# The modulation in the first feed-forward: one step behind each tile, the split's subtractions on VectorE, VectorE's order written out

## The chip, the cores and the metric

The kernel runs on one core of one Trainium2 chip. The metric is the device time of one execution in microseconds, the median of several runs. The core has five engines that take their own instructions in order: TensorE (PE; PEld is its weight load), VectorE (DVE), ScalarE (ACT), GpSimd (POOL) and SyncE (SP), which issues the loads.

## What is computed

Two transformer blocks on 512 tokens of 1024 features, in float32. The first block takes its norms' shifts, scales and gates from a vector `c`:

```python
c_act = jax.nn.silu(c)
mod = c_act @ w_mod[l] + b_mod[l]                       # 1024 x 9216
sh1, sc1, ga1, sh2, sc2, ga2, sh3, sc3, ga3 = jnp.split(mod, 9, axis=-1)
h = modulate(rms_norm(x, g_ffn1[l]), sh1, sc1)
x = x + 0.5 * (1 + ga1) * swiglu(h, w1_gate[l], w1_up[l], w1_down[l])   # D_FF = 2816
h = modulate(rms_norm(x, g_mix[l]), sh2, sc2)
x = x + (1 + ga2) * hybrid_mixer(h, ...)
h = modulate(rms_norm(x, g_ffn2[l]), sh3, sc3)
x = x + 0.5 * (1 + ga3) * swiglu(h, w2_gate[l], w2_up[l], w2_down[l])
```

The second block (a mixer and 64 experts) is not touched.

## The kernel before

Activations lie transposed, features in the partitions, 512 tokens in the columns. Every float32 product is made of three (`mm3`, L73): both operands are split in a high and a low part. A weight panel is loaded into `wraw`, ScalarE rounds it to `wh` (L105) and GpSimd subtracts, `wl` (L110); there are four buffers of each. The hidden size 2816 is 22 tiles of 128, f = 0 to 21, in four groups (0 to 5, 6 to 11, 12 to 16, 17 to 21). In `ffn` (L473) a tile is two times 24 products of 512 columns, gate and up, into PSUM (`at`, six banks). ScalarE takes the silu of the gate (L504), VectorE multiplies by the up half (L505), ScalarE makes the high part `ah` (L87), VectorE the low part `al` (L88). After a group come its down products: eight feature tiles, each 3 products per hidden tile, added to `xT` by VectorE (L517). The products of tiles 0 and 1 are made earlier, in `first_norm`.

The first feed-forward also computes seven of the nine chunks of the modulation, in 14 halves of 512 columns; such a half is called an item here. `between(f)`, called behind each tile from f = 2 on, does one: `load_mod` (L230) loads 2 MB of `w_mod` in two tiles `wmod` (four buffers); `mod_rows` (L240) sums over the eight feature tiles with c as a factor, one operation L255 and seven L257 on VectorE, in `modacc`; `thirds` (L260) splits the sum in three bfloat16 parts:

```python
nc.scalar.activation(parts[0], x, AF.Copy)
nc.gpsimd.tensor_sub(x, x, parts[0])
nc.scalar.activation(parts[1], x, AF.Copy)
nc.gpsimd.tensor_sub(parts[2], x, parts[1])
```

and `mod_cols` (L270) sums these over the partitions with twelve products of one column on TensorE, adds the bias (L280) and makes A (L285) or G (L287) of it. The gates G of the first feed-forward (the first two items) are needed by its first down products.

Within `ffn` of the first feed-forward no order is written out: a scheduler sets the order on each engine from the order in the code and what it reckons to be ready. On VectorE it lets the row operations of several items run ahead of the tile that they stand behind in the code.

Of the kernel before, what the change touches and what calls it, by code (L numbers as in the profile page):

```python
# [17 lines left out]
P = 128  # L18
# [7 lines left out]
# rows of the table of per-feature vectors, 128 features a row  # L26
# [8 lines left out]
class Net:  # L35
# [37 lines left out]
    def mm3(self, out, lh, ll, rh, rl, start, stop, open_=False):  # L73
        """float32 product from operands split in two 12-bit parts."""
        self.mm(out, lh, rh, start, False, open_)
        self.mm(out, lh, rl, False, False, open_)
        self.mm(out, ll, rh, False, stop, open_)

    def split(self, h, l, src, scale=None, pool=False):
        """h + l = scale * src, in two 12-bit parts; pool: the second on GpSimd (src in SBUF)."""  # L80
# [12 lines left out]
    def panel(self, loads, cols=1024, into=None):  # L93
        """Weights of up to [128, 1024] from DRAM, split for mm3."""
# [18 lines left out]
    def kpanel(self, src, nk, nc_, into=None):  # L113
        """src: [nk*128, nc_] in DRAM -> ([128, nk, nc_]) x 2"""
# [7 lines left out]
    def setup(self):  # L122
# [10 lines left out]
        # one table set with both Exp and Ln  # L133
        nc.scalar.preload_act_table_set("natural_log_exp_and_others")

    def load_rows(self, lo, hi):
        """Rows lo to hi of the table of vectors"""
# [13 lines left out]
    def columns(self, rows, lo, hi):  # L151
        """Rows of the table, transposed"""
# [4 lines left out]
    def silu_c(self, pool, cr):  # L157
        """silu(c) with 31 columns of zeros after each"""
# [3 lines left out]
        # c / (1 + exp(-c))  # L162
# [11 lines left out]
    def transpose_x(self, xr, j, into):  # L174
        """Feature tile j of natural tiles (in two halves), transposed"""
# [7 lines left out]
    def copy(self, i, out, src):  # L183
        """On ScalarE and VectorE in turn"""
        if i % 2:
            self.nc.scalar.activation(out, src, AF.Copy)
        else:
            self.nc.vector.tensor_copy(out, src)
# [5 lines left out]
    def in_order(self):  # L194
        """Every engine takes the block's instructions in the order they are written in."""
# [4 lines left out]
    def order(self, n0, only=None):  # L200
        """Issue order for what was traced since n0, of all engines or of one"""
# [10 lines left out]
    def behind(self):  # L212
        """What is traced in the block comes after all that was traced before, on each engine."""
# [6 lines left out]
    def scale_x(self, pool, xr, t, xs):  # L220
        """A tile of x / rms(x), natural"""
# [18 lines left out]
    def mod_rows(self, pool, rs, on_pe=False):  # L240
        """Half of the columns of one of the nine chunks of silu(c) * w_mod, to be summed over the partitions."""
        nc = self.nc
        acc = self.sb(pool, [P, 512], F32, "modacc", 2)
        if on_pe:
            # the four column groups of the array take two of the eight feature tiles each
# [14 lines left out]
    def thirds(self, pool, x):  # L260
        """Three bfloat16 parts of x"""
        nc = self.nc
        parts = [self.sb(pool, [P, 512], BF16, f"third{i}", 2) for i in range(3)]
        nc.scalar.activation(parts[0], x, AF.Copy)
        nc.gpsimd.tensor_sub(x, x, parts[0])
        nc.scalar.activation(parts[1], x, AF.Copy)
        nc.gpsimd.tensor_sub(parts[2], x, parts[1])
        return parts

    def mod_cols(self, chunk, half, parts):  # L270
        """The sums of all parts, transposed, + b_mod; A = gain * (1 + scale) and G = (1 + gate) or half of it"""
# [17 lines left out]
    def rstd(self, ssum, n, width, parts=P, r=None):  # L289
        """1 / sqrt(ssum / n + eps)"""  # L290
# [6 lines left out]
    def newton(self, r, ssum, n, t, u):  # L297
        """A step towards 1 / sqrt(ssum / n + eps): r * (1.5 - 0.5 * (ssum / n + eps) * r^2)"""
# [7 lines left out]
    HALVES = (slice(0, 256), slice(256, 512))  # L306

    def square(self, j, half, acc):
        """acc += xT[j] ** 2"""
# [7 lines left out]
    def norm_half(self, half, acc, acol, bcol, off, hs, between=lambda j: None):  # L317
        """hidden = rms(xT) * acol + bcol, split; written from column off of the hidden tiles."""
# [21 lines left out]
    def norm_after(self, steps, ahead, acol, bcol, off=0):  # L340
        """steps[half]: (j, function that updates that half of xT[j]). Returns the hidden tiles, of which the
        first half of the tokens is there, and a function that makes the second."""
# [14 lines left out]
    def pe_order(self):  # L357
        """The products from norm_after's first on, in the order they are written in"""
        self.order(self.pe_order_from, mybir.EngineType.PE)

    def use_exp(self):
        """The one table set with both Exp and Ln, for all that follows"""
# [6 lines left out]
    def first_norm(self, pool, wg, wu):  # L369
        """The first norm and modulation, in two halves of the features, and the first products, which take the first  # L370
        half while the second's modulation comes in. Returns the hidden tiles and the products."""
# [101 lines left out]
    def ffn(self, pool, i, wg, wu, wd, nxt, hs=None, second=None, between=lambda f: None):  # L473
        """hs, second: hidden tiles from norm_after; nxt: the next norm's columns. Returns the next norm_after."""
        nc = self.nc
        groups = ((0, 6), (6, 12), (12, 17), (17, 22))
        if i == 0:
            hs, done = self.first_norm(pool, wg, wu)
        else:
# [8 lines left out]
            self.pe_order()  # L488
        for f0, f1 in groups:
# [32 lines left out]
            if f1 < NF:  # L522
                for j in range(KD):
                    down(j, load(j), slice(0, S))
        self.use_exp()
        # the panels of the last four stay for the second half of the tokens
# [13 lines left out]
    def mixer_consts(self, pool):  # L540
        """Triangles, masks and selectors that depend on positions alone."""
# [5 lines left out]
        # tri[j', j] = -1 where j' >= j  # L547
# [4 lines left out]
        # ones within a head of 64, for two heads  # L552
# [6 lines left out]
        # query i (partition), key j: 0 where j <= i  # L559
# [4 lines left out]
        # key j (partition), query i: 0 where i > j  # L564
# [4 lines left out]
        # sel[32*part + h, h, :] = 1  # L569
# [11 lines left out]
    def values(self, pool, hs, w, c0, tag, second=None):  # L581
        """Natural [token, 512 features] of hidden @ w[:, c0:c0+512], the two parts of a head's 64 side by side"""
# [1499 lines left out]
```

## Time and profile before

| | |
|---|---|
| three runs | 2341.15, 2341.27, 2341.89 us; median 2341.27 |
| profiled execution, span | 2341.2 us |
| TensorE busy | 2111.6 us, 90% |
| VectorE, ScalarE, GpSimd busy | 886.0, 596.2, 649.5 us |
| first feed-forward's tiles and down products, about 44 to 456 us of the span: TensorE busy | 377.4 of 411.6 us |

The profiled execution's own time is its span, and it stands 0.1 us from the median. Busy time is the union of an engine's instructions; an instruction's time includes what it stands still inside. A wait is the idle time in front of an instruction, put down to what ended it.

### The profile page before, as it was taken

How to read it: one execution, taken by the hardware profiler on the slowest of the kernel's cores; microseconds unless marked ns; L12 is line 12 of the kernel's file. 1: busy time of each engine (PE TensorE's matmuls, PEld its weight loads, DVE VectorE, ACT ScalarE, POOL GpSimd, SP SyncE). 2: the span in 40 equal slices, each digit the busy share in tenths (PEclk: the TensorE clock that was granted, in tenths of full speed). 3: DMA queues.
4: the chain of work that ended last, by engine and by line, in shares of the span. 5: the costliest groups of instructions: out<-in, count | busy, mean ns of one | idle time of the engine just before them, and what ended most of it. 6: DMA issues, size and time to landing. Idle time of an engine off the chain costs nothing.

```text
span 2341.2 us, 28454 instructions
## 1 busy us (share of the span) xinstructions
PE 2111.6 (90%) x11561; PEld 1387.7 (59%) x11561; DVE 886.0 (38%) x1390; ACT 596.2 (25%) x1027; POOL 649.5 (28%) x415
## 2 busy tenths in 40 slices
PE   8899899899888999999899999988888599888886
PEld 5677788788767888888897764333333143333332
DVE  5958322757588522122735562111111111111112
ACT  4322222455265322223434430000000000000002
POOL 2655444575532444444535400000000000000001
PEclk9999999999999999999999999999999799999998
DMA  9676323321211232332432099999999999999998
GB/s 327 218 247 210 96 81 88 106 64 47 72 45 37 78 103 86 104 89 85 108 87 86 15 364 399 420 421 420 421 421 421 377 421 421 420 421 421 420 421 310
DMA packets 275915, 550.05 MB, mean 235 GB/s; under 512 B 18461, under 2 KB 199862, under 8 KB 228678
## 3 DMA queue, kind: packets, MB, share of 16 engines
q1 hardware_dynamic: 272832, 547.78, 62.2%
q8 instruction: 92, 1.51, 0.3%
q10 hardware_dynamic: 2950, 0.43, 0.1%
q14 instruction: 41, 0.34, 0.0%
HBM read 546.06 MB, written 2.10 MB: 234 GB/s over the span
## 4 chain that ended last, share of the span: by engine, by line
PE 47%; DMA 36%; DVE 11%; ACT 3%; issue 2%; POOL 1%; SPq 0%; POOLq 0%; ACTq 0%; DVEq 0%
PE at L71 32%; PE mm L71 15%; DMA ew<-in_expert_w_gate 12%; DMA ew<-in_expert_w_down 11%; DMA ew<-in_expert_w_up 11%; DVE modacc L257 3%; DMA wmod<-in_w_mod 1%; DVE tmp L314 1%; DVE tmp L329 0%; POOL wl L110 0%; DVE al L88 0%; DVE hl L337 0%; DVE hd L88 0%; DVE pd L690 0%; DVE pc L689 0%
## 5 line engine op out<-in xcount | busy, mean ns | idle before, releaser
L110 POOL TENSOR_TENSOR wl<-wraw,wh 128x1024 fp32r<-128x1024 f32 (+3 forms) x216 | 476.2, 2207 | 512.6 <-ACT wh L105 491.7
L71 PE MATMUL at<-ew,xg 128*32 128x512 f32 x2048 | 330.6, 644 | 72.7 <-DMA ew<-in_expert_w_up 45.9
L71 PE MATMUL at<-hh,wh 128*128 128x512 f32 (+3 forms) x800 | 301.4, 381 | 3.2 <-ACT hh L420 2.4
L71 PE MATMUL at<-hl,wh 128*128 128x512 f32 (+3 forms) x800 | 301.0, 381 | 2.3 <-DVE hl L337 2.3
L105 ACT ACTIVATE wh<-wraw 128x1024 fp32r<-128x1024 f32 (+2 forms) x193 | 183.8, 954 | 456.5 <-PE mm L71 161.4
L71 PE MATMUL at<-hh,wl 128*128 128x512 f32 (+3 forms) x800 | 299.0, 379 | 0.0
L1779 POOL TENSOR_TENSOR sg<-oh,Gt 128x512 f32<-128x512 f32 x16 | 16.8, 1047 | 853.2 <-PE at L1831 507.5
L71 PEld LDWEIGHTS at<-ew,xg 128*32 128x32 f32 x2048 | 74.9, 116 | 285.6 <-issue 139.4
L71 PE MATMUL at<-ew,ehT 128*32 128x512 f32 (+1 forms) x1040 | 185.2, 596 | 19.3 <-ACT ehT L1843 10.4
L71 PE MATMUL mm<-ah,wh 128*128 128x512 f32 (+1 forms) x432 | 155.7, 360 | 36.0 <-ACT ah L87 20.2
L71 PEld LDWEIGHTS at<-hh,wh 128*128 128x128 f32 (+1 forms) x800 | 150.8, 189 | 37.1 <-ACT hh L420 4.8
L71 PEld LDWEIGHTS at<-hl,wh 128*128 128x128 f32 (+1 forms) x800 | 151.1, 189 | 32.6 <-DVE hl L337 3.0
L71 PEld LDWEIGHTS at<-hh,wl 128*128 128x128 f32 (+1 forms) x800 | 151.8, 190 | 28.7
L71 PEld LDWEIGHTS at<-oh,xn 128*128 128x128 f32 x1024 | 123.2, 197 | 72.9 <-issue 70.5
L71 PE MATMUL mm<-al,wh 128*128 128x512 f32 (+1 forms) x432 | 154.5, 358 | 1.8 <-DVE al L88 1.8
L71 PE MATMUL at<-oh,xn 128*128 128x128 f32 x1024 | 135.3, 287 | 21.1 <-DMA ew<-in_expert_w_gate 19.7
L71 PE MATMUL mm<-ah,wl 128*128 128x512 f32 (+1 forms) x432 | 153.6, 355 | 0.0
L1866 DVE TENSOR_TENSOR ewa<-ewa,mm 128x512 f32<-128x512 f32 (+1 forms) x124 | 83.0, 670 | 168.5 <-PE mm L71 168.4
L1838 DVE SCALAR_TENSOR_TENSOR eh<-at,rslot,eh 128x512 f32<-128x512 f32 x16 | 17.4, 1085 | 324.3 <-PE at L71 324.3
L71 PE MATMUL mm<-ey,sgT 128*128 128x512 f32 (+1 forms) x264 | 125.0, 604 | 2.0 <-DVE ewa L1869 0.8
L505 DVE TENSOR_TENSOR silu<-at,silu 128x512 f32<-128x512 f32 x44 | 30.3, 689 | 253.6 <-PE at L71 245.7
L1791 DVE TENSOR_TENSOR xg<-at,gexp 128x512 f32<-128x512 f32 x31 | 21.5, 692 | 274.9 <-PE at L71 274.9
(483 smaller groups left out, 3203.1 us busy)
## 6 DMA issues: line engine op xcount, KB each, us to landing
ew<-in_expert_w_gate SPq DMA_DIRECT2D x128, 1024.0 KB, 19.8
ew<-in_expert_w_up SPq DMA_DIRECT2D x128, 1024.0 KB, 19.8
ew<-in_expert_w_down SPq DMA_DIRECT2D x122, 1024.0 KB, 19.8
wmod<-in_w_mod SPq DMA_DIRECT2D x36, 1024.0 KB, 8.2
wraw<-in_w_gate SPq DMA_DIRECT2D x44, 512.0 KB, 3.9
wraw<-in_w_up SPq DMA_DIRECT2D x44, 512.0 KB, 3.9
wraw<-in_w_in SPq DMA_DIRECT2D x39, 512.0 KB, 3.8
wraw<-in_w_down SPq DMA_DIRECT2D x40, 320.0 KB, 3.1
```

The source lines that it names most:

```text
L71: self.nc.tensor.matmul(out, lhsT, rhs, start=start, stop=stop, skip_group_check=open_)
L105: self.nc.scalar.activation(h[:, :cols], r[:, :cols], AF.Copy)
L110: (eng or self.nc.gpsimd).tensor_sub(l[:, :cols], r[:, :cols], f32(h[:, :cols]))
L257: nc.vector.scalar_tensor_tensor(acc, r, c, acc, op0=ALU.mult, op1=ALU.add)
L314: self.nc.vector.tensor_add(acc, acc, sq)
L505: nc.vector.tensor_mul(s, ps[1], s)
L1779: nc.gpsimd.tensor_tensor(sg.rearrange("p t (e s) -> p t e s", s=self.CAP), ov, self.G[:, :, es_].unsqueeze(3).to_broadcast(shp), op=ALU.mult)
L1791: nc.vector.tensor_tensor(xg[:, half * 4:half * 4 + 4], px.rearrange("p (j c) -> p j c", c=P), gain, op=ALU.mult)
L1838: nc.vector.scalar_tensor_tensor(hf, pu, rs, hf, op0=ALU.mult, op1=ALU.mult)
L1866: nc.vector.tensor_add(self.acc[t][:, cs], self.acc[t][:, cs], pc[:, :w])
```

## The change

`thirds` goes. A new function `modulation` does an item in three steps, behind three tiles one after the other: row operations, ScalarE's parts and the first subtraction behind tile f; the second subtraction behind the next tile; `mod_cols` behind the one after. Both subtractions are on VectorE. The loads of an item are written behind the row operations of the item before it, those of the first behind tile 0. Items start behind tiles 1 to 4, 6 to 10, 12 to 15 and 17; behind 5, 11, 16, 20 and 21 no item starts, but what is under way goes on. In the first feed-forward VectorE's instructions from tile 0 to the last tile's are held in the order in which they are written. Comments and docstrings have gone from the file too, and lines have moved: L505 is now L524, L517 L536, L265 L280, L267 L271, L264 L279, L266 L281, L280 L296, L285 L301, L287 L303.

```diff
-    def thirds(self, pool, x):
-        nc = self.nc
-        parts = [self.sb(pool, [P, 512], BF16, f"third{i}", 2) for i in range(3)]
-        nc.scalar.activation(parts[0], x, AF.Copy)
-        nc.gpsimd.tensor_sub(x, x, parts[0])
-        nc.scalar.activation(parts[1], x, AF.Copy)
-        nc.gpsimd.tensor_sub(parts[2], x, parts[1])
-        return parts
+    def modulation(self, pool, todo):
+        nc = self.nc
+        loads, split, cols = [self.load_mod(pool, *todo[0])], [], []
+
+        def step(start=True):
+            if cols:
+                self.mod_cols(*cols.pop(0))
+            if split:
+                chunk, half, x, parts = split.pop(0)
+                nc.vector.tensor_sub(parts[2], x, parts[1])
+                cols.append((chunk, half, parts))
+            if start and todo:
+                chunk, half = todo.pop(0)
+                x = self.mod_rows(pool, loads.pop(0))
+                if todo:
+                    loads.append(self.load_mod(pool, *todo[0]))
+                parts = [self.sb(pool, [P, 512], BF16, f"third{i}", 2) for i in range(3)]
+                nc.scalar.activation(parts[0], x, AF.Copy)
+                nc.vector.tensor_sub(x, x, parts[0])
+                nc.scalar.activation(parts[1], x, AF.Copy)
+                split.append((chunk, half, x, parts))
+
+        return step
...
     def ffn(self, pool, i, wg, wu, wd, nxt, hs=None, second=None, between=lambda f: None):
...
+        if i == 0:
+            n0 = len(self.traced())
         for f0, f1 in groups:
...
+        if i == 0:
+            self.order(n0, mybir.EngineType.DVE)
         self.use_exp()
...
                 def between(f):
-                    if f > 1 and rest:
-                        c, h = rest.pop(0)
-                        n.mod_cols(c, h, n.thirds(p, n.mod_rows(p, n.load_mod(p, c, h))))
+                    if f < 1:
+                        steps.append(n.modulation(p, rest))
+                        return
+                    steps[0](f not in (5, 11, 16, 20, 21))
```

How the instructions stand at three places. First VectorE at the end of the first group, from the row operations ahead of tile 5's product to the first `xT` of the down products. Before:

```order
L255 TENSOR_SCALAR modacc_1361<-wmod_1357,ccol_153 128x512
L257 SCALAR_TENSOR_TENSOR modacc_1361<-wmod_1357,ccol_153,modacc_1361 128x512 x3
L257 SCALAR_TENSOR_TENSOR modacc_1361<-wmod_1359,ccol_153,modacc_1361 128x512 x3
L505 TENSOR_TENSOR silu_935<-at_910,silu_935 128x512
L280 TENSOR_TENSOR mod_61<-mm_962,cols_68 128x4
L257 SCALAR_TENSOR_TENSOR modacc_1361<-wmod_1359,ccol_153,modacc_1361 128x512
L88 TENSOR_TENSOR al_939<-silu_935,ah_938 128x512
L285 SCALAR_TENSOR_TENSOR A_3_63<-mod_61,cols_68 128x4
L255 TENSOR_SCALAR modacc_1464<-wmod_1460,ccol_153 128x512
L257 SCALAR_TENSOR_TENSOR modacc_1464<-wmod_1460,ccol_153,modacc_1464 128x512 x2
L517 SCALAR_TENSOR_TENSOR xT_27_124<-mm_983,G_5_65,xT_27_124 128x512
```

And now:

```order
L255 TENSOR_SCALAR modacc_862<-wmod_767,ccol_153 128x512
L257 SCALAR_TENSOR_TENSOR modacc_862<-wmod_767,ccol_153,modacc_862 128x512 x3
L257 SCALAR_TENSOR_TENSOR modacc_862<-wmod_769,ccol_153,modacc_862 128x512 x4
L280 TENSOR_TENSOR modacc_862<-modacc_862,third_198_875 128x512
L524 TENSOR_TENSOR silu_943<-at_918,silu_943 128x512
L88 TENSOR_TENSOR al_947<-silu_943,ah_946 128x512
L296 TENSOR_TENSOR mod_61<-mm_950,cols_68 128x4
L301 SCALAR_TENSOR_TENSOR A_3_63<-mod_61,cols_68 128x4
L271 TENSOR_TENSOR third_200_877<-modacc_862,third_199_876 128x512
L536 SCALAR_TENSOR_TENSOR xT_27_124<-mm_972,G_5_65,xT_27_124 128x512
```

The product of tile 5 (`silu`) stood behind seven of the eight row operations of the sixth item; now it stands behind those of the fourth and behind that item's first subtraction. Row operations no longer stand among the `xT`.

Second ScalarE in the middle of the second group, from one tile's second part (`third`) or `ah` to the next tile's. Before:

```order
L264 ACTIVATE third_330_1681<-modacc_1672 128x512
L87 ACTIVATE ah_1456<-silu_1453 128x512
L266 ACTIVATE third_331_1682<-modacc_1672 128x512
L105 ACTIVATE wh_1705<-wraw_1703 128x1024
L504 ACTIVATE silu_1557<-at_1532 128x512
L105 ACTIVATE wh_1736<-wraw_1734 128x1024
```

And now:

```order
L279 ACTIVATE third_277_1360<-modacc_1347 128x512
L281 ACTIVATE third_278_1361<-modacc_1347 128x512
L105 ACTIVATE wh_1605<-wraw_1603 128x1024
L87 ACTIVATE ah_1431<-silu_1428 128x512
L105 ACTIVATE wh_1678<-wraw_1676 128x1024
L523 ACTIVATE silu_1531<-at_1475 128x512
```

`ah` stood right behind the first part; now the second part and a panel's `wh` stand ahead of it, and a second panel's right behind it.

Third SP, behind the last load of `first_norm` (`wmod_122`); `wraw` are weight panels, the first two those of tile 2. Before:

```order
L236 DMA wmod_122<-in_w_mod 128x4x512
L97 DMA wraw_561<-in_w_gate 128x8x128
L97 DMA wraw_592<-in_w_up 128x8x128
L236 DMA wmod_630<-in_w_mod 128x4x512
L236 DMA wmod_632<-in_w_mod 128x4x512
L97 DMA wraw_665<-in_w_gate 128x8x128
```

And now:

```order
L236 DMA wmod_122<-in_w_mod 128x4x512
L236 DMA wmod_554<-in_w_mod 128x4x512
L236 DMA wmod_556<-in_w_mod 128x4x512
L236 DMA wmod_574<-in_w_mod 128x4x512
L236 DMA wmod_576<-in_w_mod 128x4x512
L97 DMA wraw_584<-in_w_gate 128x8x128
L97 DMA wraw_615<-in_w_up 128x8x128
```

Four loads of 1 MB for the first two items stand ahead of tile 2's weights, where two stood behind them.

## Rows read from the trace of the kernel before

**Rows 1.** Waits of TensorE, 44 to 470 us: line, waited for, total, times, longest.
```profile
PE mm L71 <- ACT ah L87: 20.2, 2, 10.7
```
**Rows 2.** Timeline of TensorE: start, length, what; the second and third groups' ends.
```profile
239.99 0.79 PE L71 MATMUL mm<-ah,wh 128*128 128x512 f32 x1 [9.59 <-ACT ah L87]
...
329.47 0.39 PE L71 MATMUL mm<-ah,wh 128*128 128x512 f32 x1
```
**Rows 3.** Windows behind the first group's wait: PE, PEld, DVE, ACT, POOL busy, PEclk, DMA.
```profile
122.00:128.00 6.00, 5.94 (x15) 4.40 (x16) 5.89 (x9) 2.00 (x4) 4.37 (x3) 0.55 1.04 359
128.00:134.00 6.00, 6.00 (x27) 4.56 (x25) 5.89 (x6) 1.02 (x2) 2.93 (x2) 1.00 0.32 94
```
**Rows 4.** Timeline of VectorE, one tile of the second group.
```profile
198.90 0.68 DVE L505 TENSOR_TENSOR silu<-at,silu 128x512 f32<-128x512 f32 x1
...
200.28 0.69 DVE L88 TENSOR_TENSOR al<-silu,ah 128x512 fp32r<-128x512 f32 x1 [0.42 <-ACT ah L87]
202.04 2.62 DVE L255 TENSOR_SCALAR modacc<-wmod,ccol 128x512 f32<-128x512 f32 x1 [1.07 <-POOL third L267]
204.70 8.28 DVE L257 SCALAR_TENSOR_TENSOR modacc<-wmod,ccol,modacc 128x512 f32<-128x512 f32 x7
212.89 0.68 DVE L505 TENSOR_TENSOR silu<-at,silu 128x512 f32<-128x512 f32 x1
```
**Rows 5.** Timeline of VectorE from 79 us.
```profile
79.45 2.90 DVE L88 TENSOR_TENSOR al<-silu,ah 128x512 fp32r<-128x512 f32 x1
...
84.55 3.10 DVE L257 SCALAR_TENSOR_TENSOR modacc<-wmod,ccol,modacc 128x512 f32<-128x512 f32 x4
```
**Rows 6.** Timeline of GpSimd in the tile of rows 4.
```profile
200.84 1.17 POOL L267 TENSOR_TENSOR third<-modacc,third 128x512 bf16<-128x512 f32 x1 [5.55 <-ACT third L266]
201.96 4.95 POOL L110 TENSOR_TENSOR wl<-wraw,wh 128x1024 fp32r<-128x1024 f32 x2
```
**Rows 7.** Timeline of GpSimd beside rows 5.
```profile
78.94 5.67 POOL L110 TENSOR_TENSOR wl<-wraw,wh 128x1024 fp32r<-128x1024 f32 x2
```
**Rows 8.** Groups of ScalarE by form, 49.7 to 241 us: count, busy, mean ns, idle.
```profile
L105 ACT ACTIVATE wh<-wraw 128x1024 fp32r<-128x1024 f32 x20 | 21.0, 1054 | 28.6 <-PE mm L71 13.5 <-issue 8.0 <-PE at L71 6.4
L105 ACT ACTIVATE wh<-wraw 128x768 fp32r<-128x768 f32 x12 | 10.0, 834 | 10.9 <-PE mm L71 6.9 <-issue 4.0
L87 ACT ACTIVATE ah<-silu 128x512 fp32r<-128x512 f32 x12 | 7.5, 628 | 58.1 <-DVE silu L505 58.1
```
**Rows 9.** Groups of GpSimd by form, 300 to 357 us, with little on VectorE.
```profile
L110 POOL TENSOR_TENSOR wl<-wraw,wh 128x640 fp32r<-128x640 f32 x8 | 12.6, 1570 | 23.5 <-ACT wh L105 23.5
L110 POOL TENSOR_TENSOR wl<-wraw,wh 128x1024 fp32r<-128x1024 f32 x5 | 12.0, 2397 | 7.6 <-ACT wh L105 7.5
```
**Rows 10.** Timeline of GpSimd at 139 us.
```profile
139.15 1.84 POOL L110 TENSOR_TENSOR wl<-wraw,wh 128x768 fp32r<-128x768 f32 x1 [2.40 <-ACT wh L105]
```
**Rows 11.** Timeline of TensorE, tile 1's last products.
```profile
57.87 1.09 PE L71 MATMUL at<-hh,wl 128*128 128x512 f32 x4
```
**Rows 12.** Timeline of VectorE: `al` of tiles 5, 6 and 11, products of tiles 6 and 12.
```profile
122.04 0.69 DVE L88 TENSOR_TENSOR al<-silu,ah 128x512 fp32r<-128x512 f32 x1
...
167.16 0.69 DVE L505 TENSOR_TENSOR silu<-at,silu 128x512 f32<-128x512 f32 x1 [10.45 <-PE at L71]
...
169.03 1.97 DVE L88 TENSOR_TENSOR al<-silu,ah 128x512 fp32r<-128x512 f32 x1 [1.12 <-ACT ah L87]
...
239.97 0.69 DVE L88 TENSOR_TENSOR al<-silu,ah 128x512 fp32r<-128x512 f32 x1 [0.43 <-ACT ah L87]
...
283.63 0.69 DVE L505 TENSOR_TENSOR silu<-at,silu 128x512 f32<-128x512 f32 x1 [10.46 <-PE at L71]
```
**Rows 13.** Timeline of SP from 23 us.
```profile
23.31 5.86 SPq L236 DMA_DIRECT2D wmod<-in_w_mod  x2
29.26 2.18 SPq L97 DMA_DIRECT2D wraw<-in_w_gate  x1
```
**Rows 14.** The page's DMA issues: KB each, median us to landing.
```profile
wmod<-in_w_mod SPq DMA_DIRECT2D x36, 1024.0 KB, 8.2
```

More of the change, by code (lines that the diff above doesn't have):

```diff
@@ L476, in ffn @@
         groups = ((0, 6), (6, 12), (12, 17), (17, 22))
+        n0 = None
         if i == 0:
@@ L2017, in block_kernel @@
                 rest = [(c, h) for c in (2, 4, 3, 5, 7, 6, 8) for h in (0, 1)]
+                steps = []
                 def between(f):
-                    if f > 1 and rest:
-                        c, h = rest.pop(0)
-                        n.mod_cols(c, h, n.thirds(p, n.mod_rows(p, n.load_mod(p, c, h))))
+                    if f < 1:
+                        steps.append(n.modulation(p, rest))
+                        return
+                    steps[0](f not in (5, 11, 16, 20, 21))
                 norm = n.ffn(p, 0, a["w1_gate"][0], a["w1_up"][0], a["w1_down"][0], (n.A[1], n.mod[:, 24:32]),
```

## The prediction

> **What bounds the kernel now.** I read the waits of TensorE first, over the stretch that the change touches. Nearly all that it loses in the first feed-forward is one kind of wait: 20.2 us in two waits for ScalarE's high part `ah` of a hidden tile [rows 1]. The timeline of TensorE shows where: the second is 9.59 us long, at the end of the second group of tiles, when the down products stand before its last tile; at the end of the third group (329.47) there is none [rows 2]. The windows add what such a wait costs afterwards: in the 6 us behind the first one the granted clock is 0.55, mostly the lower level (1.2 of 2.4 GHz), and 15 products stand there where the next 6 us at 1.00 hold 27 [rows 3]. So a group's end costs about 10 us of waiting and 12 products of 0.23 us, 2.8 us, more.
>
> The wait is VectorE's. One tile of its timeline, product `silu` (198.90) to the next (212.89), takes 13.99 us [rows 4], where TensorE needs 48 products of 0.23 us and the twelve small ones, about 11.5. The eight row operations L255 and L257 should take 0.45 and 7 times 0.78 us (four in 3.10 us where nothing disturbs them [rows 5]), 5.95 in all; they took 10.9. GpSimd's rows of the same microseconds say why [rows 6]: each operation that reads two SBUF tiles stands still while a GpSimd operation runs. `al`, 0.69 us alone, took 2.90 beside the first of two panel parts that together took 5.67 [rows 5, 7]. The product `silu`, which reads PSUM, keeps its 0.68.
>
> **What the change moves.** Work is only moved: 14 items (half chunks of the modulation) as before. 28 subtractions leave GpSimd (1.17 us undisturbed [rows 6]) and come to VectorE, where I take a tile operation of the same shape, 0.69 us [rows 4]; the bfloat16 output isn't shown there, so 0.5 to 1.2 is the bound. ScalarE's 28 passes stay. VectorE's fixed order forbids what the scheduler did before: items during the down products. All 14 now lie in tile time, 4, 5, 4 and 1 to a group. A group's last tile starts no item, but its own product still stands behind the item that the tile before it started.
>
> One tile's ledger, counted from the last row operation, lengths from [rows 4 to 10]. ScalarE's first part takes 0.63 and a handoff: 0.74. VectorE's first subtraction follows: 1.42. The next tile's `silu` product comes right behind, until 2.0. ScalarE's order is now second part, a panel's high part, `ah`: 2.1, then 1.05 for a 1024-column panel [rows 8] (engines overlap by 0.1), 3.05, then `ah`, 3.6. GpSimd starts that panel's low part at 3.1 and, at 2.40 alone [rows 9], holds the operands' path until 5.5. `al` is asked for at 3.65, so it ends at 6.05 (0.55 after the GpSimd operation, as at 79.45 [rows 5, 7]). ScalarE's next panel is ready by then; its low part takes 2.85 with the wait for `al` [rows 7], to 8.3. The second subtraction ends at 8.85, the row operations, now alone, at **14.8**. The same ledger on the kernel before gives the 13.99 that is measured: two panel parts and one split part fell on its row operations. With 768-column panels (0.83 and 1.84 us [rows 8, 10]) a cycle is 13.65, mixed 14.35, with 640 columns (1.57 [rows 9]) 13.0, mixed 14.05. A cycle is so 0.8 us longer than before: GpSimd's pauses now fall where VectorE waits for ScalarE, not where it needs the path.
>
> What the trace has no row for is how the new order meets GpSimd. From below, the operations that need the path fill it without a hole: 5.95 + 3 times 0.6 + 2 times 2.40 = 12.55 us (12.0 mixed, 11.45 at 768 columns). From above, 14.8 and, if both panel parts met row operations besides, some 0.5 more. I take 14.8: it is worked out from each engine's written order, and the method gives the measured tile. The Trainium skill, page "SBUF — State Buffer", section "Who interferes with whom", says that a VectorE instruction with two SBUF inputs and a GpSimd instruction that reads SBUF exclude each other for the whole of the instruction; the stretched rows agree. By that rule alone, which counts holders and no order, the sum would be the 12.55 and speak for this change; by the rows it is 14.8.
>
> *First group.* Tile 1's products end at 58.96 [rows 11] and VectorE starts item 1 only behind its `al`; before, it had begun at 50. Four panel parts follow one another on GpSimd from about 57.8 (ScalarE: `silu`, two panels of 1.05). `al` of tile 1 ends behind the second, 63.15; three row operations are let through one per part (2.8 each), 71.5; five more, 75.4. Product of tile 2 at 76.75 (75.4 + 1.35), of tile 5 after cycles of 14.8, 14.35 and 13.65, at 119.55, its `al` 4.0 later at 123.55. Before, `al` ended at 122.73 [rows 12]: **+0.8**. TensorE also waits at some tiles' ends for the twelve small products; that lies inside the same wait.
>
> *Second group.* From tile 6's product (167.16): `al` ends 3.85 later, as before [rows 12]; row operations 5.95 with one panel part of 2.40 in them, and 1.35: 13.65. Then 14.8, 14.8, 14.35, 13.65: tile 11's product at 71.25, `al` at 75.25. Before: 240.66 − 167.16 = 73.5 [rows 12]. **+1.75**.
>
> *Third group.* Before, TensorE never waited: from tile 12's product (283.63 [rows 12]) it came to the first product that needs tile 16 at 329.47 + 12 times 0.23 = 332.2 [rows 2], 48.6 later. Now four items stand there: 13.65 + 14.8 + 14.05 + 13.0 = 55.5, `al` 3.7 later at 59.2. **+10.6**, and the lower clock behind it, **+2.8**. In the fourth group one item at its first tile is worked off before the end: 0.
>
> *Queues.* SP now has four loads of 1 MB, not two behind tile 2's weights, ahead of tile 2's weights. Two of them held SP for 5.86 us, and those weights were issued at 29.26 [rows 13]; with 10 to 16 us added and a landing of 8.2 us, as of a load of 1 MB [rows 14], they are there at 47 to 54, wanted by ScalarE at about 56.7. If later, tile 2's products still end some 5 us before VectorE takes them: 0. Later loads of w_mod stand ahead of weights and wait for VectorE's row operations, but a tile and a half ahead of use: 0. ScalarE's two panels behind `silu` of tile 1 start tile 2 about 1 us late: inside the first wait.
>
> Sum: 0.8 + 1.75 + 10.6 + 2.8 = 16 us on a span of 2341.2, which is the median of the runs (2341.27) but for 0.1: **2357 us**. The mixers and experts behind start later by the same.
>
> **The rivals.** *Path alone* (faster): GpSimd's panel parts slip into VectorE's pauses, cycles at the lower bound. Then tile 5's `al` is at 76.75 + 36.0 + 2.1 = 114.85 (−7.9), the second group 13.65 + 12.55 + 12.55 + 12.0 + 11.45 + 2.1 = 64.3 (−9.2), the third 13.65 + 12.55 + 11.75 + 11.3 + 2.1 = 51.35 (+2.75); both low clocks go, −5.6: 20 us, 2321. For it: of the 13.99 us before, 13.7 were held by some operation (0.6 for `al`, 5.95, two parts of 2.40, two of 1.17). Against it: ScalarE takes a panel just ahead of each `ah`, so its low part always gets the path first. It decides once a cycle is 1.6 us shorter than mine (ten such cycles pay for 16 us), 13.2. The Trainium skill's page "SBUF — State Buffer", same section, states the rule behind this rival. With all that lies between 2321 and the draw it has 0.26.
> *A draw*: cycles of about 13.2, the gain of two groups eaten by the third: 2341 within 5. 0.14.
> *Late weights* (slower still): tile 2's weights come more than 5 us late through SP, 5 to 8 us on top: 2363. 0.06, on the short margin of 3 to 10 us.
>
> **How the numbers follow.** About 0.2%, 4.7 us, is what a measurement of this kernel can tell from no change. My forecast (2346 to 2364) has 0.54, late weights 0.06: slower 0.60. The draw is same, 0.14; path alone and the half-way cases faster, 0.26, of which under half lies below 2326. The range from 2326 to 2364 leaves out about 0.11 below and 0.05 above. The forecast's own range is 2346 to 2364, from 0.9 us more or less in each of ten cycles.
>
> **What would show it.** Right: in the new profile the wait for `ah` at the third group's end appears, 5 to 10 us of it, perhaps part of it at the small products of the tiles before; the first two ends stay within 3 us of where they were; `silu` to `silu` on VectorE takes 13.5 to 15 us in tiles with an item, `al` 2 to 3 us. VectorE is idle through the down products. Wrong: a tile's cycle under 13.2 us, `al` at 0.7 us, or no wait at the third end.

## The result and the profile after

| | before | changed |
|---|---|---|
| median of the runs | 2341.58 us (2341.15 to 2342.19, 4 runs) | 2354.42 us (2353.48 to 2354.48, 4 runs) |
| profiled execution, span | 2341.2 us | 2352.7 us (own time 2354.4) |
| ratio | | 1.0051, 95% interval 1.0039 to 1.0064 |

The change makes the kernel 12.8 us, half a per cent, slower. (The device time stands 1.7 us above the span in every run that has both on record, the kernel before among them: 2342.18 against 2340.5 beside experiment 1. It is not the span itself, so the profile of before, at 2341.2, most likely shows an execution of about 2342.9 us, some 1.3 above the median.) TensorE's waits in the changed kernel, 44 to 470 us (line, waited for, total, times, longest):

```profile
PE mm L71 <- ACT ah L87: 13.8, 3, 5.8
PE mm L71 <- DVE third L271: 10.7, 7, 2.5
...
PE mm L71 <- DVE al L88: 4.3, 4, 1.4
```

The two waits for `ah` of 20.2 us [rows 1] are now three of 13.8. Beside them stand seven on the second subtraction, which the twelve small products need, and more on `al`: 28.8 us. The new one among the three is at the end of the third group, where there was none [rows 2]. In TensorE's timeline:

```profile
334.64 0.39 PE L71 MATMUL mm<-ah,wl 128*128 128x512 f32 x1
340.83 0.80 PE L71 MATMUL mm<-ah,wh 128*128 128x512 f32 x1 [5.79 <-ACT ah L87]
342.48 0.80 PE L71 MATMUL mm<-al,wh 128*128 128x512 f32 x1 [0.85 <-DVE al L88]
```

And behind it, as in [rows 3], windows with the granted clock (PE, PEld, DVE, ACT, POOL busy, PEclk, DMA share, GB/s):

```profile
342.00:348.00 6.00, 5.53 (x13) 4.37 (x14) 1.84 (x4) 0.74 (x1) 1.55 (x1) 0.50 0.34 99
348.00:354.00 6.00, 6.00 (x27) 4.80 (x27) 1.50 (x2) 1.48 (x2) 2.17 (x2) 0.99 0.34 100
```

At 0.50 (the lower level, 1.2 of 2.4 GHz) 13 products fit where 27 do at 0.99. One cycle of a tile in the second group in VectorE's timeline, from product to product:

```profile
208.36 0.68 DVE L524 TENSOR_TENSOR silu<-at,silu 128x512 f32<-128x512 f32 x1
210.61 2.48 DVE L88 TENSOR_TENSOR al<-silu,ah 128x512 fp32r<-128x512 f32 x1 [1.57 <-ACT ah L87]
...
213.09 2.21 DVE L271 TENSOR_TENSOR third<-modacc,third 128x512 bf16<-128x512 f32 x1
...
215.73 5.48 DVE L257 SCALAR_TENSOR_TENSOR modacc<-wmod,ccol,modacc 128x512 f32<-128x512 f32 x7
221.90 0.69 DVE L280 TENSOR_TENSOR modacc<-modacc,third 128x512 f32<-128x512 f32 x1 [0.69 <-ACT third L279]
222.51 0.68 DVE L524 TENSOR_TENSOR silu<-at,silu 128x512 f32<-128x512 f32 x1
```

The row operations, stretched to 10.9 us in [rows 4], are undisturbed now: 0.47 and seven in 5.48. The cycle is 14.15 us all the same, with one panel part of 1024 columns and one of 768. The tile before it in the changed kernel, with two of 1024 as in [rows 4], takes 14.72 against 13.99 there. ScalarE and GpSimd in the same cycle show why:

```profile
208.47 0.63 ACT L281 ACTIVATE third<-modacc 128x512 bf16<-128x512 f32 x1 [0.76 <-DVE modacc L280]
209.01 1.04 ACT L105 ACTIVATE wh<-wraw 128x1024 fp32r<-128x1024 f32 x1
209.96 0.61 ACT L87 ACTIVATE ah<-silu 128x512 fp32r<-128x512 f32 x1
```

```profile
210.13 4.62 POOL L110 TENSOR_TENSOR wl<-wraw,wh 128x1024 fp32r<-128x1024 f32 x2 [9.54 <-ACT wh L105]
```

`ah` stands behind the second part and a panel, so VectorE is idle for 1.57 us. GpSimd then takes both panel parts just as `al` and the second subtraction are asked for, and each of these (0.68 us alone) lasts until a panel part is over.

### The profile page after: what moved, and what is told of

It reads as the page before. It is cut to its first block, busy times and chain, and to the rows that moved or that the text cites. A ratio compares the mean times of both kernels' runs of the same rounds, so it can differ in the third digit from the quotient of the medians.

```text
span 2352.7 us, 28392 instructions
## 1 busy us (share of the span) xinstructions
PE 2124.3 (90%) x11561; PEld 1395.4 (59%) x11561; DVE 897.0 (38%) x1418; ACT 595.7 (25%) x1027; POOL 609.2 (26%) x387
## 4 chain that ended last, share of the span: by engine, by line
PE 40%; DMA 34%; DVE 7%; ACT 3%; issue 1%; POOL 0%; SPq 0%; POOLq 0%; ACTq 0%; DVEq 0%
PE at L71 27%; PE mm L71 13%; DMA ew<-in_expert_w_gate 12%; DMA ew<-in_expert_w_down 12%; DMA ew<-in_expert_w_up 11%; DVE tmp L330 1%; DVE tmp L345 0%; DVE hl L353 0%; DVE hd L88 0%; DVE pd L711 0%; DVE pc L710 0%; DVE smax L853 0%; ACT wh L105 0%; ACT pc L861 0%; DVE pc L866 0%
## 5 line engine op out<-in xcount | busy, mean ns | idle before, releaser
L71 PE MATMUL mm<-ah,wh 128*128 128x512 f32 (+1 forms) x432 | 157.9, 366 | 25.0 <-ACT ah L87 13.8
L71 PEld LDWEIGHTS at<-ew,ehT 128*32 128x32 f32 x1040 | 46.5, 110 | 129.5 <-issue 80.5
```

The costliest lines, as they stand in the source:

```text
L71: self.nc.tensor.matmul(out, lhsT, rhs, start=start, stop=stop, skip_group_check=open_)
```

## The experiments

Each ratio is against runs of the kernel before on the same chip, with its 95% interval. The runs come from different chips, on which the kernel before took 2341.58, 2342.48 (runs 1 to 4) and 2342.37 us (runs 5 to 8), and each interval is 2 to 3.5 us to either side: a difference between two runs of less than some 4 us is, by this estimate, not told from none.

### 1. The order on VectorE left free

```diff
-        if i == 0:
-            self.order(n0, mybir.EngineType.DVE)
```

> The changed kernel without the fixed order on VectorE; splits on VectorE, steps and one load ahead are kept. My theory: the loss comes from the fixed order, which puts 13 of the 14 row-operation chains ahead of a following tile's product and puts none into the down products. With the scheduler free, chains move into the down products again as before, and the time is 2336 us (2330 to 2343), with the silu products of a group 12.3 to 13.3 us apart where no chain stands between. Rival (splits on VectorE or the late starts themselves cost the time, the order does not matter): 2350 to 2358 us, tile cycles of 14 to 15 us as in the changed kernel.

Measured: **2326.87 us**, ratio 0.9932 (0.9918 to 0.9945). The order, and with it the placement that it fixes, costs 27.5 us, and the rest of the change gains 15. My theory's sign holds, its size was short by 9 us. VectorE in a tile of the second group:

```profile
210.29 0.69 DVE L524 TENSOR_TENSOR silu<-at,silu 128x512 f32<-128x512 f32 x1
...
211.16 0.68 DVE L280 TENSOR_TENSOR modacc<-modacc,third 128x512 f32<-128x512 f32 x1
211.76 0.68 DVE L88 TENSOR_TENSOR al<-silu,ah 128x512 fp32r<-128x512 f32 x1
212.60 0.69 DVE L271 TENSOR_TENSOR third<-modacc,third 128x512 bf16<-128x512 f32 x1 [0.15 <-ACT third L281]
...
213.85 8.42 DVE L257 SCALAR_TENSOR_TENSOR modacc<-wmod,ccol,modacc 128x512 f32<-128x512 f32 x7
222.19 0.68 DVE L524 TENSOR_TENSOR silu<-at,silu 128x512 f32<-128x512 f32 x1
```

The same work with panels of 768 columns takes 11.90 us, where the changed kernel's cycle of that kind takes 13.5. The row operations are stretched (8.42 us against 5.48), the waits are gone in this tile. Not every cycle is shorter: with two panels of 1024 columns, from tile 8's product to tile 9's, one with a chain takes 15.30 us here and 14.72 in the changed kernel. But the cycle before it holds no chain and takes 7.35, and from the group's first product to its last 61.5 us pass, with four chains among them, where the changed kernel takes 70.6 with five. The first subtraction stands between the product and `al`, where it fills the time in which ScalarE makes `ah`. Two chains started before the first tile's product, and one went among the down products of the first and of the second group. So there are two candidates for the 27.5 us, the waits and the placement; runs 4 to 6 part them.

### 2. The subtractions back on GpSimd, the order fixed

```diff
-                nc.vector.tensor_sub(parts[2], x, parts[1])
+                nc.gpsimd.tensor_sub(parts[2], x, parts[1])
...
-                nc.vector.tensor_sub(x, x, parts[0])
+                nc.gpsimd.tensor_sub(x, x, parts[0])
```

> [...] My theory: GpSimd then carries two weight parts and two slow subtractions a tile, its weight parts come later and the row operations beside it are stretched for longer: the tile cycle goes from 14.0 to 14.8 up to 15 to 16 us, time 2364 us (2357 to 2376). Rival (the splits on VectorE are what costs, because they stand ahead of the tile's product there): under 2350 us.

Order and steps are kept. Measured: **2357.66 us**, ratio 1.0062 (1.0048 to 1.0076), at the lower edge of what I expected, and not what the rival did. The theory's mechanism is not seen: GpSimd's subtractions took 1.15 to 1.18 us each here, so they are not slow, and the cycles of the second group after its first are 13.7 to 14.8 us, not 15 to 16. In the fixed order no difference between the engines is shown (3.2 us, and the intervals of the two ratios overlap): the wait for `ah` goes from 13.8 to 18.9 us, the waits on the small products from 10.7 to 4.9 (now on ScalarE's and GpSimd's parts), and 4.0 us stand on the bias addition.

### 3. The accumulator of the row operations in PSUM

```diff
-        acc = self.sb(pool, [P, 512], F32, "modacc", 2)
+        acc = self.sb(pool, [P, 512], F32, "modacc", 2) if on_pe else self.ps("mm")
```

> The changed kernel with the accumulator of the row operations in PSUM instead of SBUF, so that each of the eight row operations and the first subtraction has one operand and not two, and no result, in SBUF; all else is kept. My theory: the VectorE path of a tile (product, low part of the hidden tile, subtractions, eight row operations) is long because row operations with two SBUF operands share the way to SBUF with GpSimd and ScalarE; with the accumulator in PSUM the row operations take some 0.6 to 0.7 us each instead of 0.75 in the mean of the chain, the tile cycle falls to 12.3 to 13 us and the time to 2333 us (2325 to 2343). Rival (the operations are not stretched by a shared way; VectorE is bound by its count of operations): cycle and time stay, 2350 to 2357 us.

Measured: **2333.84 us**, ratio 0.9958 (0.9945 to 0.9972), as the theory had it. (That ScalarE has a part in the shared way, as the theory says, is shown by no run.) VectorE, and GpSimd beside it:

```profile
186.78 0.68 DVE L271 TENSOR_TENSOR third<-mm,third 128x512 bf16<-128x512 f32 x1
187.37 0.74 DVE L255 TENSOR_SCALAR mm<-wmod,ccol 128x512 f32<-128x512 f32 x1
188.15 5.51 DVE L257 SCALAR_TENSOR_TENSOR mm<-wmod,ccol,mm 128x512 f32<-128x512 f32 x7
```

```profile
187.22 2.41 POOL L110 TENSOR_TENSOR wl<-wraw,wh 128x1024 fp32r<-128x1024 f32 x1 [0.99 <-ACT wh L105]
```

With one operand in SBUF neither side loses anything: seven row operations take 5.51 us with a panel part of 2.41 on top of them. (The 0.6 to 0.7 us that I gave for one was wrong: 0.76, as with SBUF undisturbed. The gain is the missing hold, not a shorter operation.) The Trainium skill, page "SBUF — State Buffer", section "Who interferes with whom", says that a VectorE instruction with at most one SBUF input, outside the modes that use two ports, does not contend with GpSimd; for L257 and the second subtraction these rows agree. L255 reads one tile from SBUF in either kernel. It was held (2.62 us [rows 4]) where its result went to SBUF, and is not (0.74) where it goes to PSUM; in which mode it ran, no row shows. Over all 14 items the second subtraction gains most. First the changed kernel, then this run, 44 to 430 us (count, busy, mean ns of one, idle before):

```profile
L271 DVE TENSOR_TENSOR third<-modacc,third 128x512 bf16<-128x512 f32 x14 | 23.2, 1657 | 0.0
```

```profile
L271 DVE TENSOR_TENSOR third<-mm,third 128x512 bf16<-128x512 f32 x14 | 9.5, 679 | 0.0
```

The row operations L257 go from 84.2 to 74.1 us in sum, `al` from 46.5 to 41.8. Most of the waits for ScalarE stay: 21.0 us for `ah` (25.9 in the changed kernel), 9.3 for the first part (9.8). The cycle with 1024-column panels (tile 8's product to tile 9's) falls from 14.72 to 12.85. A part is given back in a new wait. I put it down to the accumulator, which now shares the two PSUM banks of the down products and the small products; that was not tried apart:

```profile
219.98 0.80 PE L71 MATMUL mm<-ah,wh 128*128 128x512 f32 x1 [4.84 <-DVE mod L296]
```

There are three such waits, 14.7 us in all.

### 4. The chains spread, the order fixed

Eight chains stay behind tiles; six are cut in pieces of two row operations (`piece`, called behind each down product; `row_ops(ks)` does the row operations `ks` of the next item).

```diff
+        def piece(j):
+            if todo:
+                row_ops(range(j % 4 * 2, j % 4 * 2 + 2))
+            if j in (1, 2) and (split or cols) or j in (3, 5, 6, 7):
+                step(j % 4 == 3)
...
                     down(j, load(j), slice(0, S))
+                    if i == 0:
+                        self.piece(j)
...
-                    steps[0](f not in (5, 11, 16, 20, 21))
+                    steps[0](f in (1, 3, 6, 8, 12, 14, 17, 18))
```

> The changed kernel with the same 14 halves of the modulation and the order on VectorE still fixed, but placed elsewhere: eight chains behind tiles 1, 3, 6, 8, 12, 14, 17 and 18, and six in pieces of two row operations behind the eight down products of each of the first three groups. My theory: a chain behind a tile costs 1.5 to 2.5 us over TensorE's 12.25 us a tile and the next tile without one gives it back; the down products of 4.7 us a piece hide two row operations of some 0.75 us each: no group ends with VectorE late, the waits before the down products (3.7, 4.4 and 5.8 us in the changed kernel, and the waits on the small products of 1 to 2.5 us) vanish or nearly so: 2316 us (2308 to 2328), below both kernels. Rival (what costs is the number of row operations on VectorE at all, or the steps' small products, wherever they stand): 2340 us or more.

Measured: **2326.44 us**, ratio 0.9929 (0.9915 to 0.9943): 28 us faster than the changed kernel, but 10 short of the 2316 that I expected. (The theory's 12.25 and 4.7 us were too long: in the changed kernel a tile without a chain takes 11.52 us and a piece of the down products 4.20.) The waits for `ah` before down products are gone, as foreseen. What I had not foreseen is a wait of TensorE on the second subtraction, which stood behind stretched row operations:

```profile
PE mm L71 <- DVE third L282: 8.4, 5, 4.0
```

### 5. The first subtraction one place later, each chain where it was

```diff
-                parts = [self.sb(pool, [P, 512], BF16, f"third{i}", 2) for i in range(3)]
-                nc.scalar.activation(parts[0], x, AF.Copy)
-                nc.vector.tensor_sub(x, x, parts[0])
-                nc.scalar.activation(parts[1], x, AF.Copy)
-                split.append((chunk, half, x, parts))
+                first.append((chunk, half, x))
...
                 nc.vector.tensor_mul(s, ps[1], s)
+                if i == 0 and f > 0:
+                    self.middle()
                 ah = self.sb(pool, [P, S], F32R, "ah", 7)
```

`middle` holds the lines that are taken out above.

> The changed kernel with VectorE's order still fixed and each chain still behind the same tile, but with the first part and the first subtraction one place later: between the next tile's product and its low part, where they stand in the run without a fixed order. In the changed kernel VectorE waits 22 times for the hidden tile's high part (25.9 us) and 14 times for the first bf16 part (9.8 us); without the fixed order 7 times (4.3 us) and 5 times (2.1 us). My theory: these hand-offs between VectorE and ScalarE, fixed one behind the other, are what the order costs: the two waits sink to under 12 us together, the tile cycle from 14.0 to 14.8 to 11.6 to 12.8 us, the time to 2329 us (2322 to 2338). Rival (the run without the order gained because chains moved ahead of the first product and into the down products): the cycle stays at 13.5 us or more and the time at 2343 us or more.

Measured: **2336.60 us**, ratio 0.9972 (0.9962 to 0.9983). The waits of VectorE (44 to 430 us), first of the changed kernel, then of this run:

```profile
DVE al L88 <- ACT ah L87: 25.9, 22, 1.6
DVE modacc L280 <- ACT third L279: 9.8, 14, 0.7
```

```profile
DVE al L88 <- ACT ah L87: 14.9, 22, 0.8
```

The second wait is gone, the first is 11.0 us shorter; 20.8 of 35.7 us are saved, and the time falls by 17.8. I had expected under 12 us to be left, and the cycles of the second group are 12.1 to 13.4 us where I gave 11.6 to 12.8. One cycle, with the panels of the cycle of 14.15 us above:

```profile
198.83 0.69 DVE L531 TENSOR_TENSOR silu<-at,silu 128x512 f32<-128x512 f32 x1
199.62 0.69 DVE L271 TENSOR_TENSOR modacc<-modacc,third 128x512 f32<-128x512 f32 x1
201.08 2.49 DVE L88 TENSOR_TENSOR al<-silu,ah 128x512 fp32r<-128x512 f32 x1 [0.78 <-ACT ah L87]
...
203.57 2.26 DVE L282 TENSOR_TENSOR third<-modacc,third 128x512 bf16<-128x512 f32 x1
...
211.66 0.68 DVE L531 TENSOR_TENSOR silu<-at,silu 128x512 f32<-128x512 f32 x1
```

12.83 us: the holds by GpSimd are unchanged (2.49 and 2.26), the 0.69 ahead of the first subtraction and half of the 1.57 ahead of `al` are gone. What is left of it has a panel of ScalarE's in it, which still stands ahead of `ah`:

```profile
199.49 1.05 ACT L105 ACTIVATE wh<-wraw 128x1024 fp32r<-128x1024 f32 x1
200.44 0.61 ACT L87 ACTIVATE ah<-silu 128x512 fp32r<-128x512 f32 x1
```

The 17.8 us are about two thirds of what the order costs. The other 9.7 us to the run without an order can lie in the 14.9 us of these waits, which are 4.3 and 2.1 there, or in the chains' places; this run does not part them.

### 6. Both: spread, and the first subtraction later

Runs 4 and 5 together, with the pieces in another order:

```diff
         def piece(j):
+            middle()
+            if j == 5:
+                step(False)
             if todo:
                 row_ops(range(j % 4 * 2, j % 4 * 2 + 2))
-            if j in (1, 2) and (split or cols) or j in (3, 5, 6, 7):
-                step(j % 4 == 3)
+            if j in (3, 7):
+                step()
```

> The kernel with the chains spread (eight behind tiles, six in pieces behind down products, order fixed), with the first subtraction one place later as in the other run of this call, and in the down products the second subtraction ahead of a piece's row operations and the small products at the eighth piece. My theory: the waits on the second subtraction (8.4 us in five places in the first spread kernel) go nearly all, and 2318 us (2311 to 2325) is left. Rival (these waits only stand in the place of others, such as weights that come late): 2324 to 2328 us, as the first spread kernel.

Measured: **2313.73 us** (4 runs), ratio 0.9876 (0.9861 to 0.9891), the fastest of all: 29 us under before, 41 under the changed kernel. The 8.4 us are down to 0.4, and no wait for `ah` is left on TensorE:

```profile
PE mm L71 <- DVE xT L569: 5.6, 4, 2.0
...
PE mm L71 <- DVE al L88: 0.9, 1, 0.9
...
PE mm L71 <- DVE third L293: 0.4, 1, 0.4
```

Chains behind tiles or spread, and the first subtraction as changed or later, make a square:

| | as changed | later |
|---|---|---|
| behind 14 tiles | 2354.4 | 2336.6 |
| spread | 2326.4 | 2313.7 |

Placement gains 28.0 or 22.9 us, the later subtraction 17.8 or 12.7 (in the lower row with the pieces' order in it).

### 7 and 8. The subtractions alone, the steps alone, no order

Run 7 is the kernel before with

```diff
-        nc.gpsimd.tensor_sub(x, x, parts[0])
+        nc.vector.tensor_sub(x, x, parts[0])
...
-        nc.gpsimd.tensor_sub(parts[2], x, parts[1])
+        nc.vector.tensor_sub(parts[2], x, parts[1])
```

and run 8 has the edits of runs 1 and 2 together.

> The kernel before, with both splitting subtractions on VectorE and nothing else changed: one part of the change alone. First theory: what the change gains without its fixed order (2326.9 us) comes from the subtractions' leaving GpSimd, whose weight parts are then earlier: 2331 us (2325 to 2335). Second theory: it comes from the steps and the loads one item ahead, and the engine of the subtractions matters little: 2341 us (2336 to 2347).

> The changed kernel without the fixed order and with both subtractions on GpSimd: the steps and the loads one item ahead alone. First theory (the subtractions' engine makes the gain): 2341 us (2335 to 2347). Second theory (steps and loads make it): 2329 us (2324 to 2334).

Measured: **2335.59 us**, ratio 0.9969 (0.9958 to 0.9980), and **2339.34 us**, ratio 0.9986 (0.9977 to 0.9995). Each lies between my two theories, nearer to the first; run 8 is in the first theory's range, run 7 just outside of both. With the free runs 1 and before:

| order | subtractions on | items as before | steps, loads ahead |
|---|---|---|---|
| free | GpSimd | 2342.4 | 2339.3 |
| free | VectorE | 2335.6 | 2326.9 |
| fixed | GpSimd | | 2357.7 |
| fixed | VectorE | | 2354.4 |

The engine gains 6.8 us, the steps 3.0, both 15.5, which is 5 to 6 us more than the sum and only just more than the intervals allow for. TensorE's wait for `ah` (44 to 470 us), 20.2 in [rows 1], is 12.4 us in run 7, 14.1 in run 8 and 8.4 in run 1.

## Why the prediction was right, point by point

**How much was tested.** The whole range, 2326 to 2364, took in faster, the same and slower, and so asks little. What the mechanism gave is 2357 (2346 to 2364), and the measured 2354.4 is 2.6 us under it; the rise itself was forecast as 16 and is 12.8 us. That the total came so near is in part luck: the terms below miss by up to 2.5 us each, and not all to one side.

**The ledger of a cycle held.** Forecast for the second group: 13.65, 14.8, 14.8, 14.35, 13.65, in all 71.25 us; the six products of VectorE stand 13.46, 14.75, 14.72, 14.15 and 13.51 apart, 70.6. In the third group 13.47, 14.75, 13.99 and 12.75 stand for 13.65, 14.8, 14.05 and 13.0. The lower bound of the path (12.55) would have needed GpSimd in VectorE's pauses; in the rows above GpSimd starts at 210.13, just ahead of `al`.

Two readings in it were too simple. Not only operations that read two SBUF tiles were held: L255 reads one and took 2.62 us [rows 4], where it takes 0.47 undisturbed. And the 20.2 us of waits for `ah` are not nearly all that TensorE lost: it was idle for 34.2 of the 411.6 us.

**The terms.** The first product of a group marks what each group added. From the changed kernel's VectorE timeline, tiles 6, 12 and 17, and the last tile's `al`:

```profile
165.43 0.69 DVE L524 TENSOR_TENSOR silu<-at,silu 128x512 f32<-128x512 f32 x1 [10.44 <-PE at L71]
...
283.93 0.69 DVE L524 TENSOR_TENSOR silu<-at,silu 128x512 f32<-128x512 f32 x1 [10.46 <-PE at L71]
...
381.45 0.69 DVE L524 TENSOR_TENSOR silu<-at,silu 128x512 f32<-128x512 f32 x1 [10.43 <-PE at L71]
...
428.13 1.27 DVE L88 TENSOR_TENSOR al<-silu,ah 128x512 fp32r<-128x512 f32 x1 [0.70 <-ACT ah L87]
```

Of before, tiles 6 and 12 are in [rows 12]; the other two:

```profile
368.93 0.69 DVE L505 TENSOR_TENSOR silu<-at,silu 128x512 f32<-128x512 f32 x1 [10.44 <-PE at L71]
...
414.81 1.27 DVE L88 TENSOR_TENSOR al<-silu,ah 128x512 fp32r<-128x512 f32 x1 [0.70 <-ACT ah L87]
```

| term | forecast | measured |
|---|---|---|
| first group, to tile 6's product | +0.8 | 165.43 − 167.16 = −1.7 |
| second group, to tile 12's product | +1.75 | 283.93 − 283.63 + 1.7 = +2.0 |
| third group with the clock behind it, to tile 17's product | +13.4 | 381.45 − 368.93 − 0.3 = +12.2 |
| fourth group, to the last `al` | 0 | 13.3 − 12.5 = +0.8 |
| behind it, in the span | 0 | 11.5 − 13.3 = −1.8 |
| from the spans to the medians | 0 | 2354.4 − 2352.7 − 0.1 = +1.6 |
| sum | +16 | +13.1 |

The largest term, 13.4, was 1.2 too large. The first group was mis-sized by 2.5: tile 2's product, taken at 76.75, came at 75.89 and tile 5's `al` ended at 122.26, not 123.55; from there to tile 6's product 43.2 us passed, where I reckoned with the 44.4 of before. The term behind the fourth group was not thought of; in the norm TensorE's wait for the low part `hl` is 1.9 us, where it was 3.4. The last row is no cost of the change: the forecast took the span of before for its device time, and as said above that profile most likely shows an execution some 1.3 us above the median. Between the two profiles the rise is 11.5 us.

**What I would look for.** The wait for `ah` at the third end is there (5.79 us), the cycles of tiles with an item lie between 12.75 and 14.75 us (I had said 13.5 to 15), `al` takes 1.6 to 2.5 us in them (I had said 2 to 3), the first two ends moved by less than 3 us, and VectorE does nothing but `xT` through the down products. By its own sign of being wrong, a cycle under 13.2 us, the 12.75 of a tile with 640-column panels would count against it; but the ledger had 13.0 for that tile, so the sign was ill put.

**Queues.** This term came out at nothing, but by a narrower margin than reckoned. The forecast has tile 2's weights issued 10 to 16 us later than at 29.26 [rows 13], and landed at 47 to 54. They were issued 21 us later, and ScalarE took the first two panels behind `silu` of tile 1 with no idle time:

```profile
50.44 0.37 SPq L97 DMA_DIRECT2D wraw<-in_w_gate  x1
```

```profile
56.03 2.00 ACT L105 ACTIVATE wh<-wraw 128x1024 fp32r<-128x1024 f32 x2
```

The first panel so landed within some 5.6 us. With the 8.2 reckoned it would have come at 58.6, behind the 56.7 when it was wanted: here the forecast was lucky. Moving these loads alone was not tried.

**The reason, tested.** The prediction said that GpSimd's pauses now fall where VectorE waits for ScalarE. Grouped by line, 44 to 430 us (count, busy, mean ns of one, idle before), first the changed kernel, then runs 1 and 6:

```profile
L257 DVE SCALAR_TENSOR_TENSOR modacc<-wmod,ccol,modacc 128x512 f32<-128x512 f32 x98 | 84.2, 859 | 3.5
...
L88 DVE TENSOR_TENSOR al<-silu,ah 128x512 fp32r<-128x512 f32 x22 | 46.5, 2113 | 25.9 <-ACT ah L87 25.9
```

```profile
L257 DVE SCALAR_TENSOR_TENSOR modacc<-wmod,ccol,modacc 128x512 f32<-128x512 f32 x98 | 115.7, 1186 | 2.7
...
L88 DVE TENSOR_TENSOR al<-silu,ah 128x512 fp32r<-128x512 f32 x22 | 21.5, 979 | 4.4 <-ACT ah L87 4.3
```

```profile
L275 DVE SCALAR_TENSOR_TENSOR modacc<-wmod,ccol,modacc 128x512 f32<-128x512 f32 x98 | 119.4, 1218 | 2.8
...
L88 DVE TENSOR_TENSOR al<-silu,ah 128x512 fp32r<-128x512 f32 x22 | 46.3, 2106 | 13.8 <-ACT ah L87 13.5
```

The slowest of the three has the shortest row operations, 859 ns: there GpSimd holds `al` (2113 ns) while ScalarE's hand-offs leave VectorE idle besides. In run 1 the panel parts fall on row operations (1186 ns), `al` is mostly free of them (979 ns) and its waits are short. So holds and hand-offs stand one behind the other in the fixed order, and taking away either helps. Run 5 moves one subtraction, takes mainly hand-offs away (`al` is held as long, 2113 ns; the second subtraction less, 1196 against 1657), and gets two thirds of the order's price back. Run 3 takes the holds of the row operations and of the second subtraction away, leaves most of the hand-offs, and gets 20.6 us back in spite of its new waits of 14.7. The two together were not tried. A held `al` alone is no loss: in run 6 it is as long as in the changed kernel (2106 ns). In run 6 a tile with a chain is mostly followed by one without, and VectorE has caught up before the group ends.

**The rival of the path alone** (2321 us; its cycle of 11.3 with 640 columns is 10.9 by its own sum, 5.95 + 1.8 + 3.14, which decides nothing) asked that GpSimd's parts should slip into VectorE's pauses. They did not in the fixed order. With the order free the kernel comes within 6 us of that time, though by another way: the hand-offs are covered and chains stand elsewhere, while the parts fall on row operations.

**What is open.** How the remaining 9.7 us between runs 5 and 1 divide between what is left of the hand-offs, the two chains ahead of the first product and those among the down products was not tried apart. The square shows that another placement, with pieces in the down products, is worth more than that.

## What to carry to other kernels

Fixing one engine's order fixes also its hand-offs to the others: when A hands to B and B back to A, put other work of A between, here the first subtraction between a product and its low part. Where another engine's operations hold this one's up, an operand in PSUM is a second way (run 3). Chains that are too long for a tile belong in pieces where the engine idles, here behind the down products. A held-up operation is no loss where nothing waits for it; look at who waits at the end of the chain, not at the mean length.

## What was not expected of the hardware

An accumulator in PSUM does not shorten an undisturbed row operation (seven in 5.51 us, against 5.48 with SBUF) and lengthens the first of a chain (L255, 0.74 against 0.47); its worth is that GpSimd's part, 2.41 us over them, holds up neither them nor the second subtraction and is itself no longer than alone (2.397 [rows 9]). With SBUF and GpSimd beside them the seven took 8.42 us in run 1. And the length of the row operations does not rank the kernels: their mean is 1218 ns in the fastest (run 6), 1255 in run 4 (2326.4 us), 859 in the changed kernel and 871 in the slowest (run 2).
